# Second feed-forward group of a streaming encoder layer: its down-projection by seven products for eight

## The chip, the cores and the metric

The kernel runs on one core of one Trainium2 chip. The metric is device time in microseconds (us), the median of several runs of the whole program.

## The reference, cut to what matters

The reference is one trunk layer for 2048 prompt tokens and 64 sample tokens (2112 in all, d_model 1024), in f32. The attention-like half (pooling and mLSTM heads) stays as it is. The change touches the second half, a gated MLP with a causal convolution of width 3:

```
h2 = rmsnorm(x, g2) * (1 + sc2) + sh2
up = h2 @ w_up                                  # 1024 -> 2 * 2816
conv = b_conv + sum(w_conv[j] * upp[:, j:j + T] for j in range(3))
a, g = jnp.split(conv, 2, -1)
x = x + gt2 * ((jax.nn.silu(g) * a) @ w_down)   # 2816 -> 1024
...
y_prompt = rmsnorm(xp, g_final)
```

## The kernel before, in words

**Tiles.** Features lie on the 128 partitions, tokens along the free dimension. The feed-forward half works through three token groups (`fgroups`, o.g = 0, 1, 2) of 704 tokens (`FT`), each seen as two halves of 352 (`FH`). d_ff is 22 blocks of 128, called f; d_model is 8 blocks, called n or k. Every f32 product is made of three TensorE passes (`PASSES`): each operand is split into a high and a low part, and high x high, high x low and low x high are added in PSUM. The split of a weight tile is one ScalarE copy (line 389) and one VectorE subtraction (line 392).

**Up-projection, all groups.** `Pair.products` makes the a and g halves of one f from seven products instead of eight (Strassen's scheme over two halves of tokens, d_model and outputs): B11, B21, T2, T3, B22, T1 and T4, each 12 matmuls of 352 columns on line 1559, so 84 for one f. Its token-side operands are the seven sums in `BN`; for group 0 they are made on the way out of the attention half, for the next groups by a generator called `prepare` (line 838 on): it reads x2 back from DRAM, applies the norm (`normed`, lines 731 and 733), forms the sums on VectorE (lines 781 to 790), splits them (lines 771 and 778), and stores them to the DRAM tile `Bd` (line 859). When the group before is at its last down-projection, `reload` brings them into SBUF (line 685). The weight-side sums come from DRAM (`wsum`; two of the four are stored already split in `wsplit` while group 0 runs, line 397, and later groups read those).

**After the products** each f goes through convolution taps (line 1547), SiLU (line 1677) and a gate (line 1684), and is split for the down-projection (`av`, lines 1703 and 1713).

**Down-projection.** In groups 0 and 1 the 22 f come in four parts (`PARTS`: 5, 5, 6, 6). After the products of a part, `down` (line 2073) multiplies all 8 n by the part's f: 6 matmuls of 352 columns for each f and n. In group 2 (`SGS`) the parts are 6, 4, 4, 4, 4 (`SPARTS`), and the first 16 f go two by two into a `Quad`: after each of the first four parts `quad_down` (line 1820) takes four f (two quads) against four pairs of n, with seven products for eight. That needs token-side sums (`b11_hi`, `t13`, `t2`, `t4` and their splits), gated values kept unsplit in `fscr` tiles, running sums in SBUF (`Y`, lines 1830 to 1850), a correction at the end (`from_quads`), and weight sums. Only the last 6 f go through `down`.

**The weight sums of the down-projection** (`down_sums`, line 1795 on) are made by DMA alone: SP copies a block of `w_quad` or of `dsum` to the DRAM tile `dsum`, then a DMA issued on POOL adds another block to it. Four j, four sums s, and four copies and four additions for each: 128 steps. `quad_down` number j needs sum j.

**What sets the order.** From line 1980 on (`manual_schedule`) the order of instructions on each engine is the order of the code. Side work lies in generators in the lists `bg[0]` to `bg[5]`; `tick(i)` runs the first generator of `bg[i]` up to its next `yield`, and `drain(i)` runs all of it at once. `bg[0]` holds the final norm of the group before (`final`), `bg[1]` holds `prepare` and `reload`, `bg[5]` holds `down_sums`. Before the change `Pair.products` has one `tick(1)` for each f; `down` has, once its list `todo` is empty, a `tick(1)` at even k and a `tick(0)` at odd k; `tick(5)` comes only in groups 1 and 2. `prepare` for group 1 runs in group 0 and `prepare` for group 2 in group 1; each has 59 yields. Weight tiles are requested by `pump` on SP's queue in the order of `stream`, up to 7 ahead, of which the first four are split (the fourth only its high part).

Of the kernel before, what the change touches and what calls it, by code (L numbers as in the profile page):

```python
# [16 lines left out]
P = 128  # L17
# [13 lines left out]
EB = 1  # L31
ENDS = ((0, 448), (448, 704))
PARTS = ((0, 5), (5, 10), (10, 16), (16, 22))
SGS = (2,)
SPARTS = ((0, 6), (6, 10), (10, 14), (14, 18), (18, 22))
NP = 8
EPS = 1e-6
# [26 lines left out]
def tile_layer(ctx: ExitStack, tc: tile.TileContext, xT, vecs, cst, rst, w_mod, w_ada, w_qkou, w_v, w_pool,  # L64
# [19 lines left out]
    def mm_ps():  # L84
        return bank("mm")
# [333 lines left out]
    class Row:  # L419


        def __init__(self):
            self.units = []
# [135 lines left out]

    x2d = dr.tile([KD, P, NTOK], F32, tag="x2d", name="x2d")  # L560
    h2d = dr.tile([KD, P, FT], F32, tag="h2d", name="h2d")
    Bd = dr.tile([len(BN), 4, P, 2, FH], F32, tag="Bd", name="Bd")
    RS2 = cp.tile([P, 32], F32, tag="RS2", name="RS2")
    pool.memset(RS2, 0.0)
    RF = cp.tile([P, 16], F32, tag="RF", name="RF")
# [98 lines left out]
    class Sums:  # L664


        def __init__(self):
            self.tiles = {}

        def make(self, nm, j):  # L670
            t = spare[0].tile([P, XT], F32R, tag="hx", name="hx", bufs=2 * len(BN))
# [7 lines left out]
        def load(self, nm):  # L679
            for j in range(2):  # L680
                t = self.make(nm, j)
                r = 0
                for v in t:
                    b, n = r % 2, v.shape[1]
                    nc.sync.dma_start(out=v.bitcast(F32), in_=Bd[BN.index(nm), 2 * j + r // 2, :, b:b + n])
                    r += n

        def at(self, nm, kc, part):
# [149 lines left out]
    def prepare(o, scr):  # L838

        box = []  # L840
        yield from bcast_cols(RS2, o.t0, FT, box, scr)
        yield
        for kc in range(4):
            for _ in range(2 if kc else 0):
                yield
            xs = [scr(), scr()]
            for x, k in zip(xs, (kc, kc + 4)):
                nc.sync.dma_start(out=x[:, :FT], in_=x2d[k, :, o.t0:o.t0 + FT])
            for _ in range(2):
                yield  # L850
            for x, k in zip(xs, (kc, kc + 4)):
                normed(x, k, o.t0, FT, box[0])
                yield

            def put(nm):
                d = scr(F32R).rearrange("p (a t) -> p a t", a=2)

                def end():
                    act.dma_start(out=Bd[BN.index(nm), kc], in_=d.bitcast(F32))
                return d[:, 0], d[:, 1], end  # L860
            yield from sums_of(xs, scr, put)

# [709 lines left out]
    class Pair:  # L1572
# [10 lines left out]
        def products(self, old):  # L1583


            o, Bo, f = self.o, self.Bo, self.f
            self.before = old
            older = old and old.before
            b1, b2 = self.b1, self.b4 = mm_ps(), mm_ps()

            def rest(*steps):
                for pair, step in steps:
                    if pair:
                        step(pair)

            def extra(i):
                for at, step in self.more:
                    if at == i:
                        step()
            rest((old, Pair.copy_u4), (older, Pair.gate))  # L1600
            product(b1, Bo, "B11", True)
            rest((old, Pair.sum_g1), (old, Pair.sum_a))
            extra(0)
            self.s1 = half_tile("s1")
            act.activation(self.s1, b1[:, :FH], AF.Copy)
            rest((older, Pair.split_hi))
            sums = o.g and not any(f == part[0] for part in (SPARTS if o.g in SGS else PARTS))
            if sums:
                tick(5)
            product(b2, Bo, "B21", True)  # L1610
            if sums:
                tick(5)
            rest((old, Pair.scale_a), (older, Pair.split_lo))
            extra(1)
            if old:
                old.last_product()
            rest((old, Pair.taps_a))
            self.ea = ext_tile(o, f, "a")
            for (a, b, d) in spans(o, 0):
                dve.tensor_tensor(out=self.ea[:, d:d + b - a], in0=b2[:, a:b], in1=self.s1[:, a:b], op=ALU.add)  # L1620
            rest((old, Pair.sum_g0))
            extra(2)
            product(b1, Bo, "T2", False)
            self.u2 = half_tile("u2")
            act.activation(self.u2, b1[:, :FH], AF.Copy)  # L1625
            rest((old, Pair.scale_g))
            if sums and o.g not in SGS:
                tick(5)
            self.b3 = mm_ps()
            extra(3)  # L1630
            product(self.b3, Bo, "T3", True)
            rest((old, Pair.taps_g))
            extra(4)
            tick(1)
            product(self.b4, Bo, "B22", True)
            rest((old, Pair.silu))
            extra(5)
            if sums:
                tick(5)
            product(b1, Bo, "T1", False)  # L1640
            if sums:
                tick(5)
# [72 lines left out]
    class Quad:  # L1715
# [68 lines left out]
        def plain(self, i, av):  # L1784

            t = f2.tile([P, XT], F32R, tag="av", name="av", bufs=6)
            d = pair_of(t, 2 * XR, FT)
            av[2 * self.p + i - PARTS[-1][0]] = lambda b, lo, hi: d[:, b, lo:hi]
            act.activation(d[:, 0], self.q[i], AF.Copy)
            return lambda: dve.tensor_tensor(out=d[:, 1], in0=self.q[i], in1=d[:, 0].bitcast(F32), op=ALU.subtract)  # L1790

    summed = []

# [14 lines left out]
    def quad_down(o, j, two, Y, first, midway):  # L1808

        for m in range(4):  # L1810
            W = Row()
            y = [Y[m][:, i * FH:(i + 1) * FH] for i in range(4)]
            a, b, c, d = (mm_ps()[:, :FH] for _ in range(4))

            def product(ps, u, i, nm, start, on=False):
                U = W.at(u)
                for k, quad in enumerate(two):
                    w = (2 * k + i) * P if u == 0 else k * P if u == 3 else (2 * i + k) * P
                    for pi, (x, z) in enumerate(PASSES):
                        pe.matmul(ps, U[:, x, w:w + P], quad.d[nm][z], start=(start and k == 0 and pi == 0),  # L1820
                                  stop=(k == 1 and pi == 2), skip_group_check=not start)
                pump()
                if todo:
                    do()
                else:
                    tick(0)

            def into(i, ps):
                if first:
                    act.activation(y[i], ps, AF.Copy)  # L1830
                else:
                    dve.tensor_tensor(out=y[i], in0=ps, in1=y[i], op=ALU.add)
            product(a, 0, 0, "B11", True)
            act.activation(d, a, AF.Copy, scale=-1.0)
            product(b, 1, 0, "T3", True)
            into(3, b)
            product(c, 1, 1, "T1", True)
            dve.tensor_tensor(out=y[3], in0=y[3], in1=c, op=ALU.subtract)
            if m == 0:
                midway()  # L1840
            product(a, 0, 1, "B21", False)
            into(0, a)
            live[0] -= 2
            product(d, 2, 0, "T2", False)
            dve.tensor_tensor(out=y[3], in0=d, in1=y[3], op=ALU.add)
            product(b, 2, 1, "B22", False)
            into(1, b)
            live[0] -= 1
            product(c, 3, 0, "T4", False)
            into(2, c)  # L1850
            live[0] -= 1
# [132 lines left out]
    for o in fgroups:  # L1984
# [3 lines left out]
        for pi, (f0, f1_) in enumerate(SPARTS if o.g in SGS else PARTS):  # L1988
# [23 lines left out]
            for f in range(f0, f1_):  # L2012
# [12 lines left out]
                while o.g in SGS and f == f1_ - 1 and not lastp and len(summed) <= pi:  # L2025
                    tick(5)
                old, pair = pair, Pair(o, Bo, f, f - f0 + nf - (f1_ - f0), av, quad, steps)
                if pi == 0 and not o.last and f == (1 if o.g else 0):
                    bg[1].append(prepare(fgroups[o.g + 1], next_scr if o.g else fscr))
                pair.products(old)  # L2030
                if o.g in SGS:
                    continue
# [25 lines left out]
            if not o.last:  # L2058
                if lastp:
                    drain(0, 1)  # L2060
                    B.append(Sums())
                    bg[1].append(reload(B[-1]))
            if lastp:
                ssum = fscr("ssum")
# [3 lines left out]
            def down(ps, W, ks, secs, stays=False):  # L2068
                for k in ks:
                    U = W.at(k // 4)  # L2070
                    for (a, b) in PASSES:
                        for i, (lo, hi) in enumerate(secs):
                            pe.matmul(ps[i][:, :hi - lo], U[:, a, k % 4 * P:(k % 4 + 1) * P], av[k](b, lo, hi),  # L2073
                                      start=(k == 0 and (a, b) == PASSES[0]), stop=(k == nf - 1 and (a, b) == PASSES[-1]))
                    if (k % 4 == 3 or k == nf - 1) and not stays:
                        live[0] -= 1
                    pump()
                    if todo:
                        do()
                    else:  # L2080
                        tick(1 - k % 2)

            def down_end(n, ps, secs):
                while Y and n not in made:
# [146 lines left out]
```

## Time and profile before

| what | us |
|---|---|
| median of 3 runs | 2201.31 (2196.95 to 2203.27) |
| the profiled execution | 2200.18 |
| its span, first to last instruction | 2198.4 |
| TensorE busy | 2173.0 (99%) |
| VectorE busy | 1630.0 (74%) |
| ScalarE busy | 1039.1 (47%) |
| GpSimd busy | 263.5 (12%) |

The profiled execution is 1.8 us longer than its span; that is what lies outside the first and last instruction. The granted TensorE clock was 0.998. In the profile PE is TensorE's matmuls, PEld its weight loads, DVE VectorE, ACT ScalarE, POOL GpSimd and SP the engine whose queue issues most DMAs. Matmuls are pipelined: one of 352 columns shows a duration of 321 ns, but a stretch of them advances by about half of that for each, so stretches are costed by their own length over their own count.

### The profile page before, as it was taken

The page shows a single profiled execution, that of the slowest core. Times are in us where ns is not written, and L with a number is a line of the kernel's source. Part 1 is how long each engine was busy: PE and PEld are TensorE (multiplying, and loading weights), DVE is VectorE, ACT ScalarE, POOL GpSimd, SP SyncE. Part 2 cuts the span into 40 slices and gives each one's busy share as a digit, 9 for nine tenths or more (in the row PEclk, how much of TensorE's full clock was granted, in tenths as well). Part 3 has the DMA queues.
Part 4 walks back from the last instruction along what each step waited for, and adds up shares of the span by engine and source line. Part 5 has one row for each costly group of instructions (what it writes and reads, how often), then busy time and mean ns, then how long its engine had stood idle before and what let it go on. Part 6 is the DMA issues. An engine that isn't in the chain of part 4 may idle for free. (4 is left out here: it accounts for less than half of the span.)

```text
span 2198.4 us, 38325 instructions
## 1 busy us (share of the span) xinstructions
PE 2173.0 (99%) x13706; PEld 2064.5 (94%) x13706; DVE 1630.0 (74%) x2999; ACT 1039.1 (47%) x2024; POOL 263.5 (12%) x546
## 2 busy tenths in 40 slices
PE   8999999999999999999999999999999999999998
PEld 7888888888899999999999999999999999999998
DVE  5887669577765768787858687776757597888885
ACT  4653334235243446464636444545435356554554
POOL 0010000001000101000100220101111331121112
PEclk9999999999999999999999999999999999999999
DMA  9967987997898696667656887767569786665562
GB/s 355 373 239 260 343 272 241 325 322 242 286 329 269 219 301 195 225 203 243 195 163 215 289 244 234 218 219 223 171 184 278 219 243 181 182 177 179 156 202 78
DMA packets 303927, 521.67 MB, mean 237 GB/s; under 512 B 27344, under 2 KB 131024, under 8 KB 303736
## 3 DMA queue, kind: packets, MB, share of 16 engines
q1 hardware_dynamic: 283320, 483.79, 67.1%
q10 hardware_dynamic: 11200, 27.04, 3.3%
q0 software_dynamic: 9216, 8.39, 2.9%
q8 instruction: 108, 1.77, 0.3%
q14 instruction: 83, 0.68, 0.1%
HBM read 408.36 MB, written 127.52 MB: 244 GB/s over the span
## 5 line engine op out<-in xcount | busy, mean ns | idle before, releaser
L1559 PE MATMUL mm<-hx,wt 128*128 128x352 f32 x5544 | 889.2, 321 | 5.7 <-DVE wt L392 3.0
L1559 PEld LDWEIGHTS mm<-hx,wt 128*128 128x128 f32 x5544 | 879.1, 188 | 10.8 <-DVE wt L392 6.4
L446 PE MATMUL mm<-hl,wt 128*128 128x512 f32 (+2 forms) x1920 | 395.8, 358 | 2.1 <-DMA wt<-hl_kept 2.1
L389 ACT ACTIVATE wt<-raw 128x512 fp32r<-128x512 f32 (+3 forms) x510 | 289.2, 579 | 210.6 <-PE mm L2073 58.8
L2073 PE MATMUL mm<-av,wt 128*128 128x352 f32 (+2 forms) x2400 | 385.0, 321 | 0.3 <-DVE av L1713 0.3
L2073 PEld LDWEIGHTS mm<-av,wt 128*128 128x128 f32 x2400 | 380.7, 188 | 2.1 <-DVE av L1713 0.6
L392 DVE TENSOR_TENSOR wt<-raw,wt 128x512 fp32r<-128x512 f32 (+3 forms) x510 | 323.8, 649 | 70.9 <-ACT wt L389 68.0
L446 PEld LDWEIGHTS mm<-hl,wt 128*128 128x128 f32 x1920 | 312.8, 188 | 49.5 <-issue 4.3
L446 PE MATMUL mm<-mx,wt 128*128 128x512 f32 (+1 forms) x960 | 186.9, 354 | 0.0
L446 PEld LDWEIGHTS mm<-mx,wt 128*128 128x128 f32 x960 | 158.9, 188 | 25.4 <-ACT mx L1417 1.1
L389 ACT ACTIVATE wt<-wt 128x512 fp32r<-128x512 f32 x176 | 110.5, 628 | 122.7 <-DMA wt<-wsum 107.2
L1547 DVE SCALAR_TENSOR_TENSOR tg<-eg,V,tg 128x704 f32<-128x704 f32 (+1 forms) x132 | 125.7, 952 | 35.0 <-ACT tg L1542 32.6
L392 DVE TENSOR_TENSOR wt<-wt 128x512 fp32r<-128x512 f32 x176 | 119.7, 687 | 33.1 <-ACT wt L389 32.5
L2090 DVE SCALAR_TENSOR_TENSOR x<-mm,MOD,x 128x352 f32<-128x352 f32 (+4 forms) x152 | 77.9, 560 | 81.0 <-PE mm L2073 81.0
L1547 DVE SCALAR_TENSOR_TENSOR ta<-ea,V,ta 128x704 f32<-128x704 f32 (+1 forms) x132 | 125.6, 951 | 7.4 <-ACT ta L1542 5.0
L1820 PE MATMUL mm<-av,wt 128*128 128x352 f32 x576 | 94.5, 321 | 0.0
L1820 PEld LDWEIGHTS mm<-av,wt 128*128 128x128 f32 x576 | 91.8, 188 | 0.0
L211 DVE SCALAR_TENSOR_TENSOR acc<-raw,CA,acc 128x512 f32<-128x512 f32 x84 | 60.5, 747 | 32.8 <-DMA raw<-w_ada 32.8
L1677 ACT ACTIVATE tg<-tg 128x704 f32<-128x704 f32 (+1 forms) x66 | 52.3, 793 | 60.8 <-DVE tg L1547 60.6
L1567 DVE TENSOR_TENSOR eg<-mm,u 128x352 f32<-128x352 f32 x154 | 69.9, 466 | 14.3 <-ACT u L1646 9.2
L1625 ACT ACTIVATE u<-mm 128x352 f32<-128x352 f32 x66 | 30.4, 461 | 92.1 <-PE mm L1559 58.2
L1153 PE MATMUL mm<-wt,hl 128*128 128x256 f32 (+1 forms) x576 | 71.0, 282 | 0.0
(330 smaller groups left out, 2284.9 us busy)
## 6 DMA issues: line engine op xcount, KB each, us to landing
wt<-hl_kept SPq DMA_DIRECT2D x108, 512.0 KB, 6.1
raw<-w_up SPq DMA_DIRECT2D x198, 256.0 KB, 4.0
wt<-wsum SPq DMA_DIRECT2D x176, 256.0 KB, 4.5
wt<-wsplit SPq DMA_DIRECT2D x88, 512.0 KB, 4.9
w<-w_up SPq DMA_DIRECT2D x88, 256.0 KB, 5.9
wsum<-w SPq DMA_DIRECT2D x44, 512.0 KB, 5.3
wsplit<-wt SPq DMA_DIRECT2D x44, 512.0 KB, 4.7
raw<-w_down SPq DMA_DIRECT2D x88, 256.0 KB, 3.7
```

Source lines behind the costliest of these rows:

```text
L211: dve.scalar_tensor_tensor(out=acc[s], in0=w, scalar=CA[:, k, s:s + 1], in1=acc[s], op0=ALU.mult, op1=ALU.add)
L389: act.activation(u.w[:, 0, :u.n], u.raw[:, :u.n], AF.Copy)
L392: dve.tensor_tensor(out=u.w[:, 1, :u.n], in0=u.raw[:, :u.n], in1=u.w[:, 0, :u.n].bitcast(F32), op=ALU.subtract)
L446: pe.matmul(ps[bi][:, :hi - lo], U[:, a, k % 4 * P:(k % 4 + 1) * P], mv[k][:, b, lo:hi], start=(at == 0 and pi == 0), stop=(k == order[-1] ...
L1153: pe.matmul(ps[ti][:n, :cols], h[4 * kh + k4][:, b, lo:lo + n], U[:, a, k4 % 2 * cols:(k4 % 2 + 1) * cols], start=(kh == 0 and k4 == 0 and ...
L1547: dve.scalar_tensor_tensor(out=t[:, :E], in0=ext[:, j:j + E], scalar=wc(j, f), in1=t[:, :E], op0=ALU.mult, op1=ALU.add)
L1559: pe.matmul(ps[:, :FH], U[:, a, kc * P:(kc + 1) * P], Bo.at(nm, kc, b), start=(first and kc == 0 and pi == 0), stop=(kc == 3 and pi == 2), ...
L1567: dve.tensor_tensor(out=ext[:, d:d + b - a], in0=ps[:, a:b], in1=u[:, a:b], op=ALU.add)
L1677: act.activation(self.tg[:, :E], self.tg[:, :E], AF.Silu)
L1820: pe.matmul(ps, U[:, x, w:w + P], quad.d[nm][z], start=(start and k == 0 and pi == 0), stop=(k == 1 and pi == 2), skip_group_check=not start)
L2073: pe.matmul(ps[i][:, :hi - lo], U[:, a, k % 4 * P:(k % 4 + 1) * P], av[k](b, lo, hi), start=(k == 0 and (a, b) == PASSES[0]), stop=(k == n ...
L2090: dve.scalar_tensor_tensor(out=x3[n][:, a:b], in0=ps[i][:, a - lo:b - lo], scalar=gt2(n, s), in1=x3[n][:, a:b], op0=ALU.mult, op1=ALU.add)
```

## The change

Group 1 joins group 2 in the seven-product form of the down-projection. With it:

- `SGS` becomes (1, 2): group 1 takes `SPARTS`, `Quad`, `quad_down` and `from_quads`.
- Both `prepare` generators are put into `bg[1]` at f = 0 of group 0, one behind the other, and both use the scratch tiles that the first one used. Each writes a DRAM tile of its own (`Bds[0]`, `Bds[1]`), and the `Sums` of a group reads its own.
- `Pair.products` has a second `tick(1)` for each f in group 0; `down` of group 0's third part has `tick(1)` at every k.
- `down` in group 0's first three parts has a `tick(5)` at every odd k, `quad_down` of group 1 has one for each pair of n, and the `tick(5)` after T2, until now only where a group was not in `SGS`, is in both later groups.
- `Quad.plain` gets a layout with the two token halves apart for a group that isn't the last.
- `final` of group 0 now waits six yields instead of three between rows, by its own rule, since group 1 is in `SGS`.

```diff
-SGS = (2,)
+SGS = (1, 2)
...
-    Bd = dr.tile([len(BN), 4, P, 2, FH], F32, tag="Bd", name="Bd")
+    Bds = [dr.tile([len(BN), 4, P, 2, FH], F32, tag=f"Bd{g}", name=f"Bd{g}") for g in range(2)]
+    Bd = Bds[0]
...
-        def __init__(self):
-            self.tiles = {}
+        def __init__(self, Bd=Bd):
+            self.tiles, self.Bd = {}, Bd
...
-                    act.dma_start(out=Bd[BN.index(nm), kc], in_=d.bitcast(F32))
+                    act.dma_start(out=Bds[o.g - 1][BN.index(nm), kc], in_=d.bitcast(F32))
...
-            if sums and o.g not in SGS:
+            if sums:
                 tick(5)
+            if o.g == 0:
+                tick(1)
             self.b3 = mm_ps()
...
-            d = pair_of(t, 2 * XR, FT)
-            av[2 * self.p + i - PARTS[-1][0]] = lambda b, lo, hi: d[:, b, lo:hi]
-            act.activation(d[:, 0], self.q[i], AF.Copy)
-            return lambda: dve.tensor_tensor(out=d[:, 1], in0=self.q[i], in1=d[:, 0].bitcast(F32), op=ALU.subtract)
+            q = self.q[i]
+            if self.o.last:
+                d = pair_of(t, 2 * XR, FT)
+                av[2 * self.p + i - PARTS[-1][0]] = lambda b, lo, hi: d[:, b, lo:hi]
+            else:
+                e = t.rearrange("p (a h t) -> p a h t", a=2, h=2)
+                d, q = e[:, :, :, :FH], self.halves(q)
+                av[2 * self.p + i - PARTS[-1][0]] = lambda b, lo, hi: e[:, b, lo // FH, :hi - lo]
+            act.activation(d[:, 0], q, AF.Copy)
+            return lambda: dve.tensor_tensor(out=d[:, 1], in0=q, in1=d[:, 0].bitcast(F32), op=ALU.subtract)
...
             if m == 0:
                 midway()
+            if o.g == 1:
+                tick(5)
...
-                if pi == 0 and not o.last and f == (1 if o.g else 0):
-                    bg[1].append(prepare(fgroups[o.g + 1], next_scr if o.g else fscr))
+                if o.g == 0 and f == 0:
+                    bg[1].extend(prepare(og, fscr) for og in fgroups[1:])
...
-                    B.append(Sums())
+                    B.append(Sums(Bds[o.g]))
...
-                        tick(1 - k % 2)
+                        tick(1 if o.g == 0 and pi == 2 else 1 - k % 2)
+                    if o.g == 0 and not lastp and k % 2:
+                        tick(5)
```

More of the change, by code (lines that the diff above doesn't have):

```diff
@@ L684, in load @@
                     b, n = r % 2, v.shape[1]
-                    nc.sync.dma_start(out=v.bitcast(F32), in_=Bd[BN.index(nm), 2 * j + r // 2, :, b:b + n])
+                    nc.sync.dma_start(out=v.bitcast(F32), in_=self.Bd[BN.index(nm), 2 * j + r // 2, :, b:b + n])
                     r += n
```

## Prediction

> **What bounds the kernel now.** I read the page first, then the windows of the three feed-forward groups, then who TensorE waits for.
>
> ```profile
> PE 2173.0 (99%) x13706; PEld 2064.5 (94%) x13706; DVE 1630.0 (74%) x2999; ACT 1039.1 (47%) x2024; POOL 263.5 (12%) x546
> ...
> L2073 PE MATMUL mm<-av,wt 128*128 128x352 f32 (+2 forms) x2400 | 385.0, 321 | 0.3 <-DVE av L1713 0.3
> ```
>
> TensorE is busy 99% of the span, so matmuls that go away shorten the kernel, as long as nothing else comes to the front. From the windows (columns: length, then busy time and count of PE, PEld, DVE, ACT, POOL, clock, DMA share, GB/s), with the borders at the first product of groups 0, 1 and 2 and the last down-projection matmul:
>
> ```profile
> 800.00:1264.10 464.10, 462.60 (x2923) 461.32 (x2921) 350.55 (x565) 242.99 (x424) 43.40 (x95) 1.00 0.68 221
> 1264.10:1733.00 468.90, 465.78 (x2926) 463.19 (x2925) 334.38 (x546) 219.74 (x390) 75.27 (x142) 1.00 0.74 223
> 1733.00:2187.00 454.00, 452.63 (x2849) 449.00 (x2848) 373.26 (x680) 241.25 (x421) 89.28 (x210) 1.00 0.59 175
> ```
>
> Group 2 already has the new form and is 14.9 us shorter than group 1. VectorE works 373 of 454 us there (82%) against 334 of 469 (71%) in group 1: the form trades TensorE time for VectorE time. Does TensorE pay for that by waiting? First two rows: group 1's weight loads; last row: group 2's (columns: total us, times, longest).
>
> ```profile
> PEld mm L1559 <- ACT s L1605: 2.1, 1, 2.1
> PEld mm L1559 <- DVE wt L392: 1.6, 4, 0.7
> ...
> PEld mm L1559 <- DVE wt L392: 2.6, 6, 0.7
> ```
>
> No. Group 2 waits 2.6 us for split weights, all told about as much as group 1 for its two reasons. The same engine load, laid out the same way, is thus seen to fit.
>
> **Part by part: matmuls.** In group 1 the 16 f that change cost 16 f x 8 n x 2 halves x 3 passes = 768 matmuls; the new form has 4 parts x 4 pairs of n x 7 products x 2 quads x 3 passes = 672. So 96 go. (The 2400 above fit: 2 x 1056 for groups 0 and 1, 288 for group 2's last 6 f.) The pace, from the chain of waits (start, length, what):
>
> ```profile
> 1899.46 23.75 PE mm L1820 x150
> ...
> 1691.36 41.85 PE mm L2073 x264
> ```
>
> 41.85 / 264 = 158.5 ns in the plain form, 23.75 / 150 = 158.3 in the new one. 96 x 158.5 ns = **15.2 us**. [...]
>
> **Group 1 as a whole.** It becomes what group 2 is, less group 2's end, where the last rows run in columns of 448 and 256 and the final norm's sums follow:
>
> ```profile
> 2141.40:2187.00 45.60, 45.60 (x289) 44.02 (x288) 28.90 (x56) 21.60 (x38) 12.35 (x11) 1.00 0.17 53
> ```
>
> The same 264 products took 41.85 us in group 1, so group 2's own end costs 3.75. Group 1 after: 454.0 - 3.75 = 450.25 us, a gain of 468.9 - 450.25 = **18.65 us**. It beats 15.2 because a wait goes with `prepare`. In the chain:
>
> ```profile
> 1368.56 8.40 DMA fscr<-x2d
> ...
> 1376.99 0.90 DVE fscr L731
> 1377.91 1.07 ACT fscr L733 x2
> 1378.98 0.36 ACT s L1605
> ```
>
> A late x2d row held the norm on VectorE and ScalarE, and behind it the ScalarE copy (L1605) that must read a PSUM bank before the next product adds to it: the 2.1 us above. The rest of the difference is smaller waits. What the new form adds in group 1 (sums, accumulations, weight splits: 16 f need 56 weight tiles' worth where 32 did) all lies inside group 2's 82%, so it is not added again. The bounds are 15.2 (group 1 keeps its waits) and 18.65 plus the 2.6 us of waits that are left, 21.2; I take 18.65, since it is read from the same code one group later. `final` of group 0, spread wider by its own rule, has the same place as `final` of group 1 has now.
>
> **Group 0 takes `prepare` for group 2.** Its size, from the instructions on the scratch tiles in group 1's later part (min/median/max ns):
>
> ```profile
> L771 ACT ACTIVATE fscr<-fscr x28: 480/487/503, 1354.8 to 1582.2; 128x352 fp32r<-128x352 f32 x28
> L778 DVE TENSOR_TENSOR fscr<-fscr x28: 519/522/529, 1355.4 to 1585.7; 128x352 fp32r<-128x352 f32 x28
> ...
> L731 DVE SCALAR_TENSOR_TENSOR fscr<-fscr,G,rbn x16: 276/581/885, 1350.8 to 1530.8; 128x640 f32<-128x640 f32 x8, 128x64 f32<-128x64 f32 x8
> ...
> L781 DVE TENSOR_TENSOR fscr<-fscr x4: 520/521/525, 1353.9 to 1545.3; 128x352 f32<-128x352 f32 x4
> ```
>
> VectorE: 28 x 0.522 + 16 x 0.581 + 16 x 0.521 (L781 is the first of four such rows) = 32.2 us, with the broadcast of the row scales about 34, over 59 yields 0.58 us each. Counting ticks: the products of the four parts of group 0 give 2 x 22 = 44, the three downs 19, 19 and 38 (a down of five f has 19 even-k ticks left once `todo` is empty, the third, at every k, 38): 120, and two generators need 119. It just fits, so the `drain` ahead of the last down finds nothing. Where the added ticks land: one more for each f in parts one to three, two in part four, 33 more in the third down (38 for 5). Is there room on VectorE?
>
> ```profile
> 828.50:867.10 38.60, 38.60 (x246) 38.60 (x245) 34.33 (x52) 25.71 (x44) 4.13 (x12) 1.00 0.71 227
> ...
> 933.70:971.70 38.00, 38.00 (x242) 38.00 (x241) 34.73 (x55) 25.65 (x44) 3.69 (x12) 1.00 0.73 233
> 971.70:1011.70 40.00, 40.00 (x255) 40.00 (x254) 30.85 (x58) 17.20 (x34) 1.24 (x4) 1.00 0.62 198
> 1038.30:1091.10 52.80, 51.59 (x326) 51.30 (x326) 47.68 (x74) 34.15 (x59) 8.08 (x16) 1.00 0.66 210
> 1091.10:1138.60 47.50, 47.50 (x301) 47.50 (x301) 27.53 (x50) 15.85 (x30) 1.28 (x4) 1.00 0.49 156
> ...
> 1165.20:1216.60 51.40, 51.40 (x327) 51.40 (x326) 44.60 (x66) 32.95 (x55) 5.02 (x16) 1.00 0.74 244
> ```
>
> The late f of each part (rows 1, 2, 4, 6) leave 4.3, 3.3, 5.1 and 6.8 us idle; they get about 3, 3, 4 and 8 ticks, 1.7, 1.7, 2.3 and 4.6 us. It fits, with VectorE at 94 to 96%. The third down (row 5) has 20.0 us idle and gets 33 x 0.58 = 19.1: nearly full, but three weight tiles stand split ahead (a tile there is 24 or 12 matmuls, so some 8 us), and the first f behind it are light. Row 3, a down with 19 ticks at 77%, lost nothing. What can't be read off is waiting (two rows of the DMA issues, then group 0's waits of SP's queue and of ScalarE):
>
> ```profile
> fscr<-x2d SPq DMA_DIRECT2D x24, 352.0 KB, 5.1
> dsum<-w_quad POOLq DMA_DIRECT2D x64, 128.0 KB, 5.1
> ...
> SPq L397 <- DVE wt L392: 119.7, 33, 7.1
> ...
> ACT fscr L771 <- DMA Bd<-fscr: 5.4, 4, 1.9
> ```
>
> In the third down, with a tick every 0.95 us (6 x 158.5 ns), two of the four pairs of x2d rows are used two ticks, 1.9 us, after their request, and take 5.1 to land: VectorE stands 3.2 us, twice, with weight splits and `down_end` queued behind it. The 8 us of cover hides one; if both add to a full VectorE, 6.4 is lost. And in the products SP already waits 119.7 us for VectorE's splits before it can store them, so a later VectorE makes later weight loads. Bounds for group 0: 0 (all covered; a gain is excluded, since only work is added) and 14.4 (6.4, and each of the 8 us that VectorE gets outside the third down and the light f). On ScalarE the moved splits wait for a scratch tile's store, 1.9 us at the longest, at half the tick rate, with weight copies behind them; ScalarE is at 52% in group 0 and gets 28 x 0.487 us and the norm, so this goes under the same cover. I take **2 us**, near the row that lost nothing. The cover, if gone, is the 6.4.
>
> **A side effect.** `next_scr` is no longer called, so the 8-column pad ahead of the tile that the B11 sums of the quads use isn't allocated, and that tile may start elsewhere.
>
> ```profile
> L1820 PE MATMUL mm<-b,wt x96: 318/322/325, 1814.3 to 2077.1; 128*128 128x352 f32 x96
> ```
>
> If each of these 96 matmuls, and of 96 more in group 1, moved by the row's own 7 ns, it would be 1.3 us either way; I take nothing.
>
> **The sums by DMA.** 56 of 128 steps move into group 0's downs; there 128-KB transfers join a DMA share of 0.49 to 0.62. Each j is ready before its use: by the end of part one 56 + 20 steps are done where 32 are needed, so the forcing loop runs empty. Group 2 no longer has any step. I cost it at nothing; cover: SP's 7 tiles ahead; the price if it is gone is the second rival.
>
> **Sum.** 2200.18 - 18.65 + 2 = 2183.5 us for an execution like the profiled one. The median of the runs lies 1.1 us above that execution, so **2185** (2184.6).
>
> **Rivals.** *Group 0 gives it back*: VectorE saturates there, 14.4 us as bounded: 2200.2 - 18.65 + 14.4 + 1.1 = 2197, no change. For: 94 to 96% and the x2d waits. Against: windows at 90% with no loss, and group 2 at 85% without. Chance 0.12.
>
> *SP's queue stops at the sums, slower.* A copy dsum<-dsum waits on SP for POOL's addition; all weight loads queue behind it. For each j two sets of copies do so, 8 in all; the tighter one follows its addition by four ticks, 4 x 12 matmuls = 7.6 us in group 0's downs, against 5.1 to land. If POOL issued so late that each set held SP for one whole landing beyond the cover, 8 x 5.1 = 41 us would go: 2185 + 41 = 2226. It decides from about 3 us for each set (23 us in all eat the gain and 0.3%). Against: the additions landed in 5.1 us with VectorE at 71 to 82%. [...] Chance 0.06.
>
> *It doesn't do what it says*: a tick fewer than counted leaves `prepare` to the drain; one to three yields cost 1 to 3 us. That stays in the range.
>
> **How the numbers follow.** Forecast 0.82, rivals 0.12 and 0.06. What this kernel's measurement can tell from no change is about 0.3%, 6.6 us: faster means under 2194.7. The range's low end is 21.2 gained at no cost and a run 2 to 3 us quicker than the profiled one, as the runs spread: 2177. Its high end is 15.2 gained, 8 lost in group 0 and the 3 us of spread: 2196. Faster 0.82, same 0.12, slower 0.06.
>
> **What would show it.** Right: L2073 falls to x1632, L1820 rises by 672; group 1 lasts about 450 us; group 0 464 to 468; VectorE over 85% in the third down with PE unbroken; the wait of L1605 for x2d gone from group 1. Wrong: TensorE waiting in group 0 for L392 by several us (first rival); SP waiting at L1801 for tens of us (second); group 1 over 455 us, which would say that group 2's order doesn't carry over.

## The result, and the profile after

The changed kernel takes 2210.55 us (median of 4 runs, 2207.98 to 2214.69) against 2199.68 for the kernel before (4 runs, 2196.95 to 2203.27): the ratio is 1.0054, 95% interval 1.0040 to 1.0068. It is slower; the forecast was 2185, faster. The profiled execution took 2207.98 us with a span of 2206.2, 7.8 us over the one before.

The page of the changed kernel: the busy times, and the two lines of the down-projection (`down` is on line 2084 now, `quad_down` on 1829, the products on 1560).

```profile
PE 2171.0 (98%) x13610; PEld 2059.9 (93%) x13610; DVE 1690.6 (77%) x3107; ACT 1073.1 (49%) x2084; POOL 266.3 (12%) x545
...
L2084 PE MATMUL mm<-av,wt 128*128 128x352 f32 (+2 forms) x1632 | 266.6, 324 | 3.4 <-DVE x L2103 3.4
...
L1829 PE MATMUL mm<-av,wt 128*128 128x352 f32 x1152 | 190.0, 321 | 0.0
```

The matmuls went as counted: 13706 - 13610 = 96, with 1632 left in the plain form and the row of `quad_down` at 1152 where it had 576. But TensorE is busy for 2171.0 us, only 2.0 less than before, though 96 x 158.5 ns is 15.2: the matmuls that are left have become longer. The windows of the three groups in the changed kernel (same columns as before the change):

```profile
799.16:1290.29 491.13, 476.21 (x2927) 471.04 (x2925) 379.31 (x629) 262.15 (x471) 63.49 (x123) 0.98 0.79 250
1290.29:1740.83 450.54, 450.30 (x2827) 449.14 (x2825) 365.91 (x591) 233.89 (x403) 72.99 (x133) 1.00 0.73 212
...
1740.80:2195.10 454.30, 453.26 (x2850) 449.80 (x2848) 373.33 (x680) 241.21 (x422) 74.44 (x190) 1.00 0.52 164
```

Group 1 takes 450.5 us where 468.9 were; it gives 18.4. Group 2 is as it was. Group 0, whose own matmuls nobody touched, takes 491.1 where 464.1 were: **27.0 us** more. Half of it is idle time of TensorE (491.1 - 476.2 = 14.9 against 464.1 - 462.6 = 1.5, so 13.4 more), half is the same number of matmuls taking longer (476.2 against 462.6, 13.6 more), at a granted clock of 0.98 instead of 1.00. Who TensorE's weight loads waited for in group 0 of the changed kernel (total us, times, longest):

```profile
PEld mm L1560 <- ACT s L1606: 7.5, 3, 3.8
PEld mm L2084 <- DVE x L2103: 4.5, 4, 3.7
PEld mm L1560 <- ACT wt L389: 4.0, 2, 3.8
PEld mm L1560 <- DVE wt L392: 2.8, 4, 1.1
```

A few long breaks, not many short ones: TensorE stands for 3.7, 3.0, 3.5 and 3.7 us (from one matmul's start to the next, less 0.16 us for the matmul itself). The first two end at L1606, the ScalarE copy `s1` of the first product of an f, which must be through before the third product adds to the same PSUM bank. ScalarE's own timeline ahead of one of them, around the end of the first down (start, length, what; in brackets the idle time before it and who ended it):

```profile
906.34 0.63 ACT L389 ACTIVATE wt<-wt 128x512 fp32r<-128x512 f32 x1 [2.08 <-DMA wt<-wsum]
906.40 0.33 ACTq L860 DMA_DIRECT2D Bd<-fscr  x1
910.25 0.50 ACT L772 ACTIVATE fscr<-fscr 128x352 fp32r<-128x352 f32 x1 [3.28 <-DMA Bd<-fscr]
910.25 0.33 ACTq L860 DMA_DIRECT2D Bd<-fscr  x1
913.26 0.50 ACT L772 ACTIVATE fscr<-fscr 128x352 fp32r<-128x352 f32 x1 [2.51 <-DMA Bd<-fscr]
913.26 0.33 ACTq L860 DMA_DIRECT2D Bd<-fscr  x1
913.66 0.61 ACT L389 ACTIVATE wt<-wt 128x512 fp32r<-128x512 f32 x1
914.34 0.50 ACT L772 ACTIVATE fscr<-fscr 128x352 fp32r<-128x352 f32 x1
914.75 0.45 ACT L1606 ACTIVATE s<-mm 128x352 f32<-128x352 f32 x1
```

This is the mechanism in nine lines. L772 is a split of `prepare`; it needs a scratch tile (`fscr`) that is free only when an earlier split's store to DRAM has landed. ScalarE takes its instructions in the order of the code: it stands for 3.28 and 2.51 us at those stores, and the copy that TensorE needs (914.75) stands behind them. Waits of 4.37, 1.27 and 1.09 us for such stores stand ahead of the second break. The other two breaks end at other lines and have the same root. For the third, inside the third down, VectorE's timeline; for the fourth, ScalarE's:

```profile
1124.51 0.53 DVE L779 TENSOR_TENSOR fscr<-fscr 128x352 fp32r<-128x352 f32 x1 [2.42 <-ACT fscr L772]
1124.95 3.03 DVE L2103 SCALAR_TENSOR_TENSOR x<-mm,MOD,x 128x352 f32<-128x352 f32 x6
```
```profile
1161.01 0.50 ACT L772 ACTIVATE fscr<-fscr 128x352 fp32r<-128x352 f32 x1 [5.38 <-DMA Bd<-fscr]
...
1162.27 0.61 ACT L389 ACTIVATE wt<-raw 128x512 fp32r<-128x512 f32 x1
```

In the third, VectorE waits for a split L772 that itself waited 2.48 us for a store, and `down_end` (L2103), which has to empty the PSUM bank, stands behind it. In the fourth, a weight split (L389) stands behind a wait of 5.38 us for a store.

Then comes the second half. TensorE's breaks and the stretches behind them, as windows:

```profile
911.60:915.20 3.60, 0.15 (x1) 0.00 (x0) 1.72 (x4) 1.87 (x5) 0.00 (x0) 1.00 0.97 374
916.70:919.90 3.20, 3.20 (x12) 3.20 (x12) 2.13 (x5) 1.78 (x4) 0.00 (x0) 0.50 0.36 147
...
1121.90:1125.50 3.60, 0.31 (x2) 0.02 (x1) 1.18 (x4) 0.81 (x3) 0.00 (x0) 0.91 1.08 357
1125.60:1131.60 6.00, 6.00 (x20) 5.79 (x21) 4.61 (x10) 1.59 (x3) 0.81 (x1) 0.50 0.96 315
```

Behind a break of 3.6 us the granted clock is 0.50, and 20 matmuls take 6.0 us where 3.2 would do. The trace's clock records have four such stretches in group 0, 3.4, 3.4, 6.8 and 6.8 us long, and none in group 0 before; TensorE worked 18.4 of these 20.5 us, so they cost 9.2 of the 13.6 us by which the matmuls became longer; most of the rest, 4.3 us, is also there in prep_only below (466.9 for 462.6), which has no such stretch, and was not traced. How idle TensorE was ahead of each of the four stands in the last section.

### The profile page after: what moved, and what is told of

The parts are those of the page before. It is cut to its first block, busy times and chain, and to the rows that moved or that the text cites. A ratio compares the mean times of both kernels' runs of the same rounds, so it can differ in the third digit from the quotient of the medians.

```text
span 2206.2 us, 38420 instructions
## 1 busy us (share of the span) xinstructions
PE 2171.0 (98%) x13610; PEld 2059.9 (93%) x13610; DVE 1690.6 (77%) x3107; ACT 1073.1 (49%) x2084; POOL 266.3 (12%) x545
## 4 chain that ended last, share of the span: by engine, by line
PE 85%; DMA 6%; DVE 5%; issue 2%; ACT 2%; SPq 1%; POOL 0%; ACTq 0%; DVEq 0%; POOLq 0%
PE mm L1560 35%; PE mm L446 23%; PE mm L1829 10%; PE mm L2084 7%; PE mm L1154 3%; DMA Bd<-fscr 2%; DVE wt L392 1%; DMA wt<-wsum 1%; PE m L1335 1%; PE m L1336 1%; PE m L1324 1%; PE m L1313 1%; DMA raw<-w_ada 1%; PE m L1416 1%; PE mm L1084 0%
## 5 line engine op out<-in xcount | busy, mean ns | idle before, releaser
L389 ACT ACTIVATE wt<-raw 128x512 fp32r<-128x512 f32 (+3 forms) x526 | 301.7, 587 | 177.9 <-PE mm L446 48.6
L392 DVE TENSOR_TENSOR wt<-raw,wt 128x512 fp32r<-128x512 f32 (+3 forms) x526 | 338.0, 657 | 65.2 <-ACT wt L389 64.2
L2084 PE MATMUL mm<-av,wt 128*128 128x352 f32 (+2 forms) x1632 | 266.6, 324 | 3.4 <-DVE x L2103 3.4
L2084 PEld LDWEIGHTS mm<-av,wt 128*128 128x128 f32 x1632 | 261.7, 190 | 6.6 <-DVE x L2103 4.5
L1829 PE MATMUL mm<-av,wt 128*128 128x352 f32 x1152 | 190.0, 321 | 0.0
L1829 PEld LDWEIGHTS mm<-av,wt 128*128 128x128 f32 x1152 | 184.8, 188 | 0.0
L389 ACT ACTIVATE wt<-wt 128x512 fp32r<-128x512 f32 x176 | 110.0, 627 | 105.5 <-DMA wt<-wsum 93.5
L1548 DVE SCALAR_TENSOR_TENSOR ta<-ea,V,ta 128x704 f32<-128x704 f32 (+1 forms) x132 | 125.5, 951 | 7.8 <-ACT ta L1543 5.0
L2103 DVE SCALAR_TENSOR_TENSOR x<-mm,MOD,x 128x352 f32<-128x352 f32 (+4 forms) x104 | 52.2, 549 | 29.2 <-PE mm L2084 29.1
```

Source lines behind the costliest of these rows:

```text
L389: act.activation(u.w[:, 0, :u.n], u.raw[:, :u.n], AF.Copy)
L392: dve.tensor_tensor(out=u.w[:, 1, :u.n], in0=u.raw[:, :u.n], in1=u.w[:, 0, :u.n].bitcast(F32), op=ALU.subtract)
L1548: dve.scalar_tensor_tensor(out=t[:, :E], in0=ext[:, j:j + E], scalar=wc(j, f), in1=t[:, :E], op0=ALU.mult, op1=ALU.add)
L2103: dve.scalar_tensor_tensor(out=x3[n][:, a:b], in0=ps[i][:, a - lo:b - lo], scalar=gt2(n, s), in1=x3[n][:, a:b], op0=ALU.mult, op1=ALU.add)
```

## The experiments

**Theory A**: late landings hold ScalarE and VectorE (stores hold ScalarE for want of scratch tiles; x2d rows hold VectorE), at places where TensorE's next operation stands right behind. **B**: the DMA sums that the change puts into group 0's downs crowd the DMA engines, so that everything lands late. **C**: VectorE is simply full in group 0. The table has the medians, the ratio to the kernel before on the same chip with its interval, and from the profiled execution the four parts of group 0, each from its first product to the next part's. A kernel with one run has no interval.

| kernel | us | ratio | part 1 | 2 | 3 | 4 | group 0 |
|---|---|---|---|---|---|---|---|
| before | 2199.68 | 1 | 107.1 | 104.6 | 127.0 | 125.5 | 464.1 |
| changed | 2210.55 | 1.0054 (1.0040 to 1.0068) | 108.6 | 110.6 | 138.9 | 133.0 | 491.1 |
| prep_only | 2205.99 | 1.0030 (1.0018 to 1.0043) | 106.6 | 106.1 | 130.4 | 128.5 | 471.7 |
| sums_only | 2201.59 (one run) | | 107.3 | 105.7 | 130.3 | 125.5 | 468.7 |
| no_sums_g0 | 2240.29 (one run) | | 108.5 | 105.1 | 131.3 | 129.5 | 474.4 |
| scratch | 2197.28 | 0.9998 (0.9987 to 1.0009) | 107.9 | 105.1 | 131.2 | 135.4 | 479.6 |
| early | 2195.75 | 0.9986 (0.9977 to 0.9995) | 107.3 | 106.7 | 130.3 | 137.0 | 481.4 |
| few_sums | 2193.54 | 0.9975 (0.9966 to 0.9984) | 107.7 | 105.3 | 129.5 | 131.8 | 474.3 |
| few_plain | 2206.01 (one run) | | 108.7 | 110.5 | 137.8 | 129.5 | 486.5 |
| best | 2190.73 | 0.9961 (0.9948 to 0.9973) | 108.3 | 106.2 | 129.3 | 129.2 | 472.9 |
| spread_plain | 2214.25 | 1.0081 (1.0065 to 1.0097) | 116.1 | 113.1 | 128.0 | 136.3 | 493.5 |
| spread | 2196.90 | 0.9993 (0.9983 to 1.0002) | 108.1 | 116.7 | 126.5 | 127.8 | 479.1 |
| best2 | 2186.15 | 0.9944 (0.9930 to 0.9957) | 106.9 | 107.0 | 126.8 | 128.4 | 469.1 |
| best2_plain | 2198.57 | 1.0000 (0.9990 to 1.0010) | 108.6 | 109.9 | 129.8 | 129.4 | 477.7 |

**scratch**: two tiles that group 0 leaves idle take the sums t and u of `prepare`, so four scratch tiles are left for splits.

```diff
-            yield from sums_of(xs, scr, put)
+            room = ["rbn", "ssum"]
+            yield from sums_of(xs, lambda: fscr(room.pop(0)), put)
```

> The changed kernel with two more scratch tiles for prepare: the sums t and u go to the tiles that group 0 leaves idle (rbn and ssum), so four of the six scratch tiles are free for splits on their way to DRAM, where two or three were. Same instructions, same ticks. Theory A (ScalarE's queue stands at the store of a scratch tile, and the copy that TensorE needs stands behind it): group 0 falls from 491 us to 466 to 474, the waits of ScalarE for Bd<-fscr (31 us in group 0) to under 8, the whole to 2184 to 2194 us. Theory B (the DMA sums in group 0's downs crowd the DMA engines, so everything lands late): group 0 stays over 480. Theory C (VectorE is full): group 0 stays at 488 to 492.

Group 0 fell by 11.5 us, the whole to 2197.3: a tie with before; group 0 lies between the bands of A (466 to 474) and B (over 480). ScalarE's waits for the stores in group 0, first the changed kernel, then this one (the same view of two kernels):

```profile
ACT fscr L772 <- DMA Bd<-fscr: 31.6, 16, 5.4
```
```profile
ACT fscr L772 <- DMA Bd<-fscr: 6.0, 4, 3.0
```

The first two parts healed and no clock stretch is left in them; a break of 2.9 us stayed in the third down, for a weight split, and one of 5.9 us at the start of the fourth part. There ScalarE stood 3.03 us at a store and then 3.75 us at a weight row (`wt<-wsum`), with the copy of the fourth part's first product behind both. So the want of scratch tiles is one cause, and late weight rows are another, as far as this trace shows.

**no_sums_g0** takes the `tick(5)` out of group 0's downs. **prep_only** is the kernel before with both `prepare` in group 0, with their ticks. **sums_only** is the kernel before with the `tick(5)` in group 0's downs.

> The changed kernel without the steps of the DMA sums in group 0's downs; all 128 steps run in group 1 and later, the first ones forced ahead of the first quad. Theory A: group 0 stays at 485 to 492 us. Theory B: group 0 falls to 466 to 474. Theory C: group 0 stays at 488 to 492. Under all three group 1 is longer than 450.5 by a few us, since its first quad waits for the forced sums.

> The kernel before with one part of the change: both prepares in group 0, with the second tick for each f and the full rate in the third down. Group 1 keeps its plain down-projection, the sums stay in groups 1 and 2. Theory A and C: group 0 487 to 492 us, group 1 464 to 467 (its own wait for x2d gone), the whole 2218 to 2226 us. Theory B: group 0 464 to 470, the whole 2195 to 2203.

> The kernel before with the other part alone: 56 steps of the DMA sums in group 0's downs, nothing else. Theory A and C: group 0 464 to 466 us, the whole 2197 to 2203 us. Theory B: group 0 475 us or more, the whole over 2208.

None of the three theories had this. B came nearest: 474.4 in no_sums_g0 and 471.7 in prep_only lie just over its bands, but sums_only, with 468.7, lies 6 us under B's 475. `prepare` alone costs group 0 7.6 us, the sums alone 4.6 (one run), both together 27.0. The median time of a store from issue to landing between 855 and 1160 us, from the DMA issues of the kernel before, the changed one, prep_only and sums_only:

```profile
Bd<-fscr ACTq DMA_DIRECT2D x28, 352.0 KB, 2.9
```
```profile
Bd<-fscr ACTq DMA_DIRECT2D x44, 352.0 KB, 4.3
```
```profile
Bd<-fscr ACTq DMA_DIRECT2D x49, 352.0 KB, 3.8
```
```profile
Bd<-fscr ACTq DMA_DIRECT2D x28, 352.0 KB, 4.4
```

So B is a half of it: the sums by themselves make a store land as late as in the changed kernel, but with half as many stores ScalarE waits far less. Its waits for them in group 0 are 5.4 us before, 8.9 in sums_only, 17.9 in prep_only and 31.6 with both, more than the two additions make together. TensorE's breaks grow with them: the longest is 2.2 us in prep_only, with full clock behind it (granted 0.999 over the whole run), and 3.0 to 3.7 us in the changed kernel, with half clock (0.50) behind each. In sums_only one break of 3.05 us had that too:

```profile
1016.60:1020.20 3.60, 0.71 (x5) 0.43 (x4) 0.73 (x2) 0.98 (x2) 0.00 (x0) 1.00 0.99 380
1020.50:1023.90 3.40, 3.40 (x14) 3.40 (x13) 0.41 (x2) 0.96 (x2) 0.00 (x0) 0.50 0.79 310
```

no_sums_g0 also shows what the steps in group 0 are for: without them the sums are forced ahead of each quad of group 1, TensorE breaks by 8.5, 7.3, 6.1 and 7.0 us there, and group 1 takes 500.4 us.

**early** is scratch, and the x2d rows are requested ahead of the idle yields instead of behind them.

```diff
-            for _ in range(2 if kc else 0):
-                yield
...
-            for _ in range(2):
+            for _ in range(4 if kc else 2):
                 yield
```

> The kernel with the two more scratch tiles, and prepare asks for its x2d rows two ticks earlier: the two idle yields stand behind the request instead of ahead of it; the number of yields stays. Theory A, now in two parts (late landings hold the two in-order engines: stores hold ScalarE, which the scratch tiles relieved, and x2d rows used two ticks after their request hold VectorE in the third down): the third and fourth parts of group 0, 131.2 and 135.4 us, fall together by 6 to 12, the waits of VectorE for fscr<-x2d from about 10 us to under 4, the whole to 2186 to 2192 us. Theory C (VectorE is full in the third down): the two parts stay at 264 or more.

A miss. VectorE's waits for x2d in group 0 went from 13.0 to 11.5 us only, and the parts stayed where they were (267.4 for 266.6). The request stands two ticks earlier in the program but not in time: SP's queue was at that place held by a weight tile not yet split. The whole, 0.14% under before, can't be told from scratch (their intervals overlap).

**few_sums** is scratch without the sums in the third down; **few_plain** is the same edit on the changed kernel; **best** is all three edits.

```diff
-                    if o.g == 0 and not lastp and k % 2:
+                    if o.g == 0 and pi < 2 and k % 2:
...
-            if o.g == 1:
+            for _ in range(3 if o.g == 1 else 0):
                 tick(5)
```

> The kernel with the two more scratch tiles, and no step of the DMA sums in the third down: 32 steps are left in group 0, and quad_down of group 1 has three for each pair of n instead of one. Theory B' (the sums' transfers make all landings later where the DMA engines are full already): the third and fourth parts fall together by 6 to 14 us, landings of Bd<-fscr there to 3.9 us, group 1 stays at 449 to 452, the whole 2184 to 2192. Theory A without B': the two parts stay within 3 us of 266.6. Theory C: the same.

> The changed kernel with its own scratch tiles and x2d requests, and only the sums taken out of the third down (three steps for each pair of n in group 1's quad_down). Theory B': third part from 138.9 to about 131 us, fourth from 133.0 to about 129, as without any sums in group 0; first two parts stay at 108 and 110. Theory A alone: third and fourth part stay within 3 us.

> All three edits: two more scratch tiles, earlier x2d requests, no sums in the third down. If late landings are the whole cause, group 0 comes to 464 to 470 us and the whole to 2181 to 2187, about what the matmuls saved; if VectorE's load counts by itself, group 0 stays at 475 or more and the whole over 2190.

few_sums: third and fourth part fall by 5.2 us together, just under B's band; the whole is 0.25% under the kernel before. few_plain: the fourth part came to 129.5 as B said, the third stayed at 137.8, where it should have fallen: with few scratch tiles the break at its start is 3.8 us, with 6.8 us at half clock behind it, and one of 2.2 us is left in the third down. best: 472.9 for group 0, between the two readings, and 2190.7, just in the second; a break of 3.0 us is left at the start of the fourth part, where ScalarE stands 3.94 us at a weight row.

**spread_plain** and **spread** move the dense `tick(1)` from the third down into the middle rows of all three (the changed kernel, and best).

```diff
-                        tick(1 if o.g == 0 and pi == 2 else 1 - k % 2)
+                        tick(1 if fast else 1 - k % 2)
...
-                    down(ps, rows[n], range(nf), secs, ends)
+                    down(ps, rows[n], range(nf), secs, ends, o.g == 0 and not lastp and n < (7 if pi == 2 else 6))
```

> The changed kernel with nothing but its tick(1) places moved: in group 0's first two downs every k of the rows 3 to 5 has one, in the third every k of the rows 3 to 6, and all other rows have theirs at even k (123 ticks where 119 are needed). So prepare runs denser in the middle of the downs and thinner in the last rows ahead of the next products; scratch tiles, x2d requests and sums as in the changed kernel. Theory A (what counts is that ScalarE and VectorE stand in front of the next part's first copy): the breaks of TensorE at the three borders fall from 3.7, 3.0 and 3.7 us to under 1.5 each, group 0 from 491 to under 480. If the scarce scratch tiles count wherever the ticks lie (B and scarcity together), group 0 stays within 5 us of 491.

> The best kernel so far (two more scratch tiles, earlier x2d requests, no sums in the third down) with the same moved ticks. Theory A: the break of 3.0 us at the border of the third down and the fourth part goes, third and fourth part together from 258.5 to 253 to 256 us, the whole from 2191 to 2185 to 2189. If VectorE's load by itself is what is left: no change, 2189 to 2193.

Both missed as wholes. Third and fourth part of spread came to 254.3 us as A expected, but its second part rose to 116.7. TensorE's timeline there:

```profile
1004.84 2.22 PE L2083 MATMUL mm<-av,wt 128*128 128x352 f32 x13
1009.82 0.66 PE L721 MATMUL m<-fscr,ones_r 128*128 128x352 f32 x1 [2.76 <-ACT fscr L715]
1010.75 0.66 PE L722 MATMUL m<-fscr,ones_r 128*128 128x352 f32 x1 [0.26 <-DVE fscr L716]
```

With the ticks moved forward, the second `prepare` begins inside the second down, and its broadcast matmuls (L721) stand in TensorE's own queue a few ticks behind the ScalarE copy that they need. One matmul of 352 columns shows 0.66 us here at a granted clock of 0.50 (in the records from 1009.27 on), where the row of `quad_down` in the changed kernel has 0.32. In spread_plain a weight split was late by 4.8 us in the first down: so with scarce scratch tiles the denser ticks moved the break and did not remove it.

**best2** instead takes three ticks out of the third down's last row alone and gives f = 10 and f = 11, right behind the second down, a third tick.

```diff
+            if o.g == 0 and f in (10, 11):
+                tick(1)
...
+                    down(ps, rows[n], range(nf), secs, ends, o.g == 0 and pi == 2 and n < KD - 1)
```

> The best kernel so far with three ticks fewer in the last row of the third down (even k only), and a third tick for f = 10 and f = 11, where VectorE is light. If prepare's steps in the last row are what holds ScalarE in front of the fourth part's first copy, the break of 3.0 us there falls to under 1.5, third and fourth part together from 258.5 to about 256 us, the whole from 2191 to 2187 to 2190. If the late weight rows there come from the DMA engines or SP's queue instead, the break stays at 2.5 to 3.5 us and the whole at 2189 to 2193.

The break at the start of the fourth part went to 1.0 us, the two parts to 255.2, the whole to 2186.15: 0.56% faster than the kernel before, and no clock stretch in group 0. Its group 0 as a window, and its group 1:

```profile
800.73:1269.79 469.06, 465.93 (x2927) 462.83 (x2925) 379.06 (x628) 262.52 (x470) 54.63 (x112) 1.00 0.77 254
1269.79:1718.90 449.11, 448.48 (x2826) 446.68 (x2825) 366.35 (x591) 233.03 (x403) 82.62 (x145) 1.00 0.75 220
```

VectorE is busy 379.06 us in group 0, in the changed kernel it was 379.31. The same VectorE work in 469.1 and in 491.1 us: theory C falls.

**best2_plain** is best2 without the scratch tiles and the earlier requests.

> The fastest kernel so far without its two scratch tiles and without its earlier x2d requests: what is left of the edits is no sums in the third down, three ticks fewer in its last row and a third tick at f = 10 and f = 11. If the scarce scratch tiles are a cause of their own (theory A), the borders of the first two downs break by about 3.5 us again, each with a stretch at half clock, and group 0 goes from 469 to 480 or more, the whole to 2197 or more. If the placement of the ticks was all, group 0 stays under 473 and the whole under 2191.

2198.57, a tie with before; group 0 at 477.7, a little under the band of A. Breaks of 3.1 and 3.0 us are back at the first two borders, the first with a stretch at half clock. ScalarE's waits for stores are 26.7 us here and 5.0 in best2. So the placement alone doesn't do it; with the scratch tiles but without the placement, best stands at 2190.7. (best2_plain lacks the earlier x2d requests too, which by themselves made 1.5 us, less than the runs can tell.)

## Why the prediction was wrong, step by step

- *96 matmuls at 158.5 ns, 15.2 us*: right in count, 13706 to 13610. The 15.2 us can't be read by themselves, since the time is read in groups, not in these 96.
- *Group 1 becomes group 2 without its end, 450.25 us*: 450.54 measured, 18.4 us gained for 18.65. Reading the price of the new form from the group that already had it was the part that held, down to its small waits.
- *The sums are ready in time, the ticks suffice*: right; nothing was forced ahead of a quad. *I cost it at nothing*: wrong. They cost 4.6 us alone, and in sums_only stores land later (4.4 us for 2.9), x2d rows too (8.2 for 3.3).
- *Group 0: 2 us, bounds 0 and 14.4*: wrong, and this is the step that failed. It measured 27.0. The sentence was that ScalarE's wait for a scratch tile, "1.9 us at the longest", would go "under the same cover". Two things were wrong in it. The 1.9 us came from a schedule with 28 splits of `prepare` in group 0, only one of them between 7 us ahead of a border of two parts and 6 us behind it; the changed kernel has 56, and three to six of them there at each border, where DMA is full (1.01 in 899.0 to 911.5). A wait was up to 5.4 us and all of them 31.6. And the cover, split weight tiles, covers only a late split, which at the fourth break it did not do either. It does nothing for the copy L1606, which is no weight and stands in ScalarE's queue behind the waiting split.
- *Below the sum, nothing for the clock*: the prediction had no term for it. 9.2 of the 27.0 us are stretches at half clock behind breaks.
- *VectorE at 94 to 96% fits*: right in the end. best2 has the same load in group 0 and does it in 469.1 us. That its 2186.15 lies 1.2 us from the forecast is not the forecast come true: it is another kernel, with more scratch tiles and other ticks.
- *First rival, group 0 gives it back*: right in place, wrong in engine and size: it named VectorE's load and 14.4 us. *Second rival, SP stands at the sums*: in the changed kernel SP's waits at the copies (L1810) come to 1.4 us in all. So the sums did harm by their traffic, not by order. Nor did the additions issued on POOL land later there: 4.9 us (median from 855 to 1160 us), against 5.1 over the whole kernel before.

What stays open: how much of the 27.0 us is the sums' traffic and how much the scratch tiles can't be given as two numbers, since the parts (7.6 and 4.6) don't add up. No run takes the steps of the sums in the first two downs out of best2, so what they still cost there isn't known. And no run holds the clock, so that its 9.2 us are read from the trace, not tried.

## What to carry to other kernels

When side work is moved, look not only at how full the engines are there but at what stands behind each of its waits in the same queue at the new place, the borders between stages above all: a ready buffer of weights is no cover for a copy that stands behind a wait. Ask of each scratch tile how long it is taken, store's landing included, and count how many are free at the new rate. On a kernel bound by TensorE, look at the granted clock behind a break before pricing it at its length alone: here four breaks of 3.0 to 3.7 us had 3.4 or 6.8 us at 0.50 behind them, which cost 9.2 us more, and one of 3.0 us in best had none.

## What the runs showed of the hardware

In group 0, breaks of TensorE of 2.2 to 6 us were in some places followed by a granted clock of 0.50 for 3.4 or 6.8 us, and in others not. In the changed kernel the stretches begin at 916.61, 1025.84, 1124.83 and 1162.37 and last 3.41, 3.41, 6.83 and 6.83 us; the starts lie 109.23, 98.99 and 37.55 us apart, which is 32, 29 and 11 times 3.413. The windows of this length that end where they begin (window, length, then TensorE's busy time):

```profile
913.20:916.61 3.41, 1.37 (x8) 1.37 (x9) 2.83 (x6) 2.91 (x6) 0.00 (x0) 1.00 0.66 262
...
1022.43:1025.84 3.41, 0.62 (x4) 0.62 (x5) 3.00 (x7) 2.32 (x6) 0.00 (x0) 1.00 0.97 383
...
1121.41:1124.82 3.41, 0.80 (x6) 0.51 (x4) 0.99 (x3) 0.89 (x3) 0.00 (x0) 1.00 1.04 381
...
1158.96:1162.37 3.41, 0.41 (x3) 0.12 (x1) 0.53 (x1) 1.00 (x3) 0.00 (x0) 1.00 1.08 324
```

Of all other windows in step with these, at full clock and between 795 and 2150 us, the emptiest has TensorE busy for 1.97 us (909.79 to 913.20), and 1.00 followed. A window of sums_only, one of few_plain, and two of best that follow each other:

```profile
1017.10:1020.51 3.41, 0.67 (x4) 0.67 (x5) 1.04 (x2) 0.98 (x2) 0.00 (x0) 1.00 1.01 402
```
```profile
1125.30:1128.71 3.41, 1.42 (x7) 1.18 (x8) 2.56 (x6) 1.43 (x3) 0.00 (x0) 1.00 0.98 372
```
```profile
1146.53:1149.95 3.42, 1.80 (x10) 1.51 (x10) 2.34 (x5) 0.00 (x0) 0.00 (x0) 1.00 1.00 321
1149.95:1153.36 3.41, 2.18 (x14) 2.18 (x15) 1.72 (x3) 2.08 (x4) 0.00 (x0) 1.00 0.93 317
```

The break of 3.05 us in sums_only lies in one window (busy 0.67 us of 3.41) and half clock followed (0.50 in 1020.5 to 1023.9). So does one of only 2.2 us in few_plain (1.42), and half clock followed. The one of 3.02 us in best is shared by two windows (1.80 and 2.18), and none followed (1.00 in 1151.2 to 1157.0). So in these records a break's length alone doesn't decide: half clock followed windows with TensorE busy for 0.41 to 1.42 us, and none of those with 1.80, 1.97 and 2.18. This is read from the records; no run moves a break and nothing else.

A transfer of 352 KB took 2.9 us at the median (855 to 1160 us) in the kernel before, 4.4 in sums_only with the same number of such stores, and 4.3 in the changed kernel, where the core's DMA engines were at 0.97 to 1.08 during the breaks.
